# RMSNorm row sums on TensorE in a two-layer network kernel: the matmuls that sum squares get stationaries of 32 columns on four groups of columns, where they had 128

## The chip, the cores and the metric

The kernel runs on one core of one Trainium2 chip. The metric is the device time of one execution in microseconds (us), lower is better. The time before is a median of 2035.81 us over three runs (2034.48 to 2036.75).

## What is computed

Two layers over 1024 tokens of 1024 features, in float32, then a last norm:

```python
for layer in range(DEPTH):                       # DEPTH = 2
    h = rmsnorm(x, mix_norm[layer])
    y = sliding_window_attention(h, ...) if layer % 2 == 0 else hgrn2_recurrence(h, ...)
    x = x + y
    h = rmsnorm(x, mlp_norm[layer])
    x = x + jnp.square(jax.nn.relu(h @ w_up)) @ w_down    # 1024 -> 4096 -> 1024
return rmsnorm(x, final_norm)
```

`rmsnorm(x, gain)` is `x * rsqrt(mean(x*x over features) + 1e-5) * gain`. The recurrence has one more such norm of its output. The mean over features, one number for each token, is what the change is about.

## The kernel before

**Layout.** Activations lie with 128 features on the partitions and 512 tokens (a half, `hf` 0 or 1) along the free axis, so one half of `x` is 8 tiles of 128x512. Matmuls on float32 data go as three float32r products (`mm3`): the data are split into a high and a low part (tiles `a`, `t` for activations, `wh` and `wl` for weights). The accumulators in PSUM are the tiles `p` and `q`, four of each. The MLPs and the recurrence's projections use Strassen products, and their operands go to DRAM (`d`) and back.

**The means.** `sum_squares` (L545) squares the eight tiles of a half on ScalarE and adds them on VectorE into one tile of 128x512: the sum over 8 features for each partition and token. `token_rstd` (L555) then has to add over the 128 partitions. It does so on TensorE, one block of 128 tokens at a time: the stationary is the block of the summed squares (128 partitions x 128 tokens), the one moving column is `self.mean`, a 128x1 tile that holds 1/1024, and the result is a column of 128 partitions in a `q` tile, the mean of squares of each token. Both operands are float32, and the trace holds two MATMUL and two LDWEIGHTS records (two passes) for each such matmul. A chain of five small VectorE and one small ScalarE instructions on 128x4 tiles (`sm`) makes 1/sqrt of it, and `spread` or a scalar operand uses it.

`token_rstd` is called 13 times: twice before the attention (`scaled`), four times in `weigh` (two for each MLP), twice for the recurrence's input (`hgrn_first`, `hgrn`), twice for its output (`hgrn_out`), each time for a half of 512 tokens and so with 4 matmuls; and three times in `final`, where the sum comes in two parts (seven tiles, then the eighth), that is 8 matmuls for the first half and 4 for each of two quarters. That makes 56 matmuls, 112 passes. In the very last call three and four matmuls of the identity with itself (`warm`, written to `q` tiles that nobody reads) stand behind the two parts.

**Matmuls with 32 columns.** The recurrence (`recurrence`) already has matmuls whose stationary has 32 columns: each writes 32 partitions of a PSUM tile, and four of them in turn write the four groups of 32 partitions. They come in visits of 64 matmuls (128 passes) or 32, four visits for each of the 8 heads, with ordinary matmuls in between.

**What sets the order.** Nothing runs when it is written: every instruction is recorded (`Schedule.add`), and `Schedule.forward` plans all engines with costs in ns that stand in the code. On each engine the ready operation of lowest rank goes next. On TensorE the rank is the place in which the operation was recorded, less a lead; on the other engines it is, from the second pass on, the latest start that `backward` finds. `order` makes four passes and keeps the plan that ends first by its own costs. A change of form, from matmuls on the whole array (`"whole"`) to matmuls on groups of columns (`"columns"`), counts 200 ns in the plan (`DRAIN`). All instructions are then issued from one line (L434), so the profile names them by tiles: the norm's matmuls are `q<-c,t 128x1` (in `hgrn_out`, `q<-c,a 128x1`), the 32-column ones of the recurrence are `q<-t,t` with 128*32.

Of the kernel before, what the change touches and what calls it, by code (L numbers as in the profile page):

```python
# [17 lines left out]
P = 128  # L18
# [24 lines left out]
QB = 32  # L43
# [5 lines left out]
class View:  # L49


    def __init__(self, buf, steps=(), part=None):
        self.buf, self.steps, self.part = buf, steps, part
# [103 lines left out]
class Schedule:  # L157


    def __init__(self):  # L160
        self.ops, self.tags, self.lead = [], {}, 0

    def tile(self, pool, bufs, shape, dtype, tag, name):
        return View(Buf(pool, bufs, shape, dtype, tag, name))
# [1 line left out]
    def add(self, ways, outs, ins, tail=0.0, form=None, table=None):  # L166

        op = Op()
        op.ways, op.tail, op.form, op.table, op.index = ways, tail, form, table, len(self.ops)
        lead = self.lead  # L170
        if any(isinstance(v, View) and v.buf.tag == "p" for v in ins):
            lead = max(lead, EVACUATE)
        op.late = None
        op.rank, op.after, op.first = (len(self.ops) - lead, len(self.ops)), [], []
        before, bufs = set(), {}
        for views, writes in ((ins, False), (outs, True)):
            for v in views:
                if isinstance(v, View):
                    bufs[v.buf] = None
                    before.update(v.buf.conflicts(v.part, writes))  # L180
        for views, writes in ((ins, False), (outs, True)):
            for v in views:
                if isinstance(v, View):
                    v.buf.note(op, v.part, writes)
        before.discard(op)
        op.bufs, op.before = list(bufs), list(before)
        op.banks = [v.buf for v in ins if isinstance(v, View) and v.buf.tag in "pq"]
        for b in op.bufs:
            if b.uses == 0:
                op.first.append(b)  # L190
                self.tags.setdefault((id(b.pool), b.tag), []).append(b)
            b.uses += 1
            b.users.append(op)
        for o in before:
            o.after.append(op)
        self.ops.append(op)
# [183 lines left out]
class Net:  # L380
# [174 lines left out]
    def token_rstd(self, acc, inner=1.0, outer=1.0, n=TH, keep=False, more=(), busy=(0, 0)):  # L555

        ps = self.psum("q")
        nb = n // P
        parts = [acc, *more]
        for i, z in enumerate(parts):  # L560
            for j in range(nb):
                first, last = (j == 0, j == nb - 1) if more else (True, True)
                self.mm(ps[:, j : j + 1], z[:, j * P : j * P + P], self.mean, i == 0 and first, i == len(parts) - 1 and last, P, 2,
                        skip_group_check=bool(more))
            if busy[i > 0]:
                self.warm(self.ident, busy[i > 0], "q", 217.0)
        v, y, z = (self.t(F32, (P, BPH), "sm")[:, :nb] for _ in range(3))
        self.ts("DVE", v, ps[:, :nb], inner, EPS, ALU.mult, ALU.add, 4)
        self.act(y, v, AF.Sqrt, 4)
        self.op("DVE", self.nc.vector.reciprocal, [y], [y], 100, y, y)  # L570
        self.tt("DVE", z, y, y, ALU.mult, 4)
        self.stt(z, v, -0.5 * outer, z, ALU.mult, ALU.mult, 4)
        if keep:
            y, r = self.const((P, BPH)), y
        else:
            r = y
        self.stt(y, z, 1.5 * outer, r, ALU.add, ALU.mult, 4)
        return y
# [1362 lines left out]
```

## Time and profile before

| | |
|---|---|
| three runs, median | 2035.81 us |
| the profiled execution's own time | 2035.75 us |
| its span, first to last instruction | 2034.0 us |
| mean granted TensorE clock | 0.998 |
| TensorE matmul (PE) busy | 2017.9 us, 99% |
| VectorE (DVE) busy | 1841.3 us, 91% |
| ScalarE (ACT) busy | 1310.6 us, 64% |
| moved to and from HBM | 243 GB/s over the span |

In the profile PE is TensorE's matmuls and PEld its loads of stationaries, which overlap them. A line of a group gives the engine, the operation, out<-in by tile names, the shape, the count, the busy time in us and the mean length of one in ns, and the idle time before them. Busy time is the union of the instructions' times, so overlapping ones share it. A line of the timeline gives the start and the length in us, then the instructions that are merged in it. Ends of matmuls are modelled and overlap the next one's start; what a matmul costs is seen from starts, not from lengths.

### The profile page before, as it was taken

The numbers are of one execution on the slowest core, as the hardware profiler recorded it, in microseconds if no ns is written. First come the engines' busy times: TensorE is split into PE (matmuls) and PEld (weight loads), VectorE is DVE, ScalarE is ACT, GpSimd is POOL, SyncE is SP. The second block draws the span as 40 slices with busy tenths as digits, with TensorE's granted clock in tenths as the row PEclk, the third lists the DMA queues.
The fourth block names the chain that finished last, engine by engine and source line by source line (L and its number), as shares of the span: only waits on it lengthen the run. The fifth ranks groups of instructions, "written<-read, shape, count | busy, mean of one in ns | idle before, by whom it ended". The sixth has DMA issues, their size and how long they took to land.

```text
span 2034.0 us, 40229 instructions
## 1 busy us (share of the span) xinstructions
PE 2017.9 (99%) x13964; PEld 1714.3 (84%) x13964; DVE 1841.3 (91%) x3738; ACT 1310.6 (64%) x2759; POOL 64.4 (3%) x152
## 2 busy tenths in 40 slices
PE   9999999999999999999999999999999999999998
PEld 7878888899998888888888888878888999888887
DVE  8899979899999979889989999989999999997985
ACT  7577977667676544657666666666767667544573
POOL 4030000000000000000000000000000000000000
PEclk9999999999999999999999999999999999999999
DMA  6212478778789987755888889979798788997812
GB/s 229 78 51 73 137 254 264 248 263 281 269 289 309 319 279 236 255 171 182 283 285 284 284 292 310 329 254 316 243 299 296 258 295 285 322 319 233 269 53 83
DMA packets 275420, 497.40 MB, mean 245 GB/s; under 512 B 30992, under 2 KB 36368, under 8 KB 275216
## 3 DMA queue, kind: packets, MB, share of 16 engines
q1 hardware_dynamic: 275072, 494.81, 72.5%
q8 instruction: 110, 1.80, 0.4%
q14 instruction: 94, 0.77, 0.1%
q10 hardware_dynamic: 144, 0.02, 0.0%
HBM read 394.57 MB, written 100.14 MB: 243 GB/s over the span
## 4 chain that ended last, share of the span: by engine, by line
PE 92%; DVE 5%; DMA 1%; ACT 1%; issue 1%; SPq 0%; DVEq 0%; ACTq 0%
PE p L434 50%; PE q L434 42%; DVE t L434 2%; DVE a L434 1%; DVE wl L434 1%; DVE m L434 1%; ACT t L434 0%; DVE sm L434 0%; DMA a<-in_x 0%; DMA d<-t 0%; DMA t<-in_x 0%; DMA d<-a 0%; ACT a L434 0%; SPq L434 0%; ACT m L434 0%
## 5 line engine op out<-in xcount | busy, mean ns | idle before, releaser
L434 PE MATMUL p<-a,wh 128*128 128x512 f32 (+1 forms) x2832 | 781.9, 361 | 1.3 <-ACT t L434 0.8
L434 PE MATMUL q<-a,wh 128*128 128x512 f32 x2020 | 626.5, 390 | 0.4 <-DVE a L434 0.2
L434 PEld LDWEIGHTS p<-a,wh 128*128 128x128 f32 x2832 | 503.3, 189 | 82.0 <-ACT t L434 1.3
L434 PE MATMUL p<-a,wl 128*128 128x512 f32 (+1 forms) x1416 | 504.1, 359 | 0.7 <-DVE wl L434 0.7
L434 PEld LDWEIGHTS q<-a,wh 128*128 128x128 f32 x2020 | 374.7, 188 | 74.9 <-DVE a L434 0.8
L434 PE MATMUL q<-a,wl 128*128 128x512 f32 x1008 | 392.0, 389 | 0.0
L434 ACT CAST wh<-m 128x512 fp32r<-128x512 f32 (+1 forms) x354 | 212.8, 605 | 204.1 <-PE q L434 96.3
L434 ACT CAST wh<-wr 128x512 fp32r<-128x512 f32 (+1 forms) x324 | 194.5, 603 | 164.8 <-PE p L434 106.8
L434 PEld LDWEIGHTS p<-a,wl 128*128 128x128 f32 x1416 | 266.5, 189 | 39.2 <-DVE wl L434 1.4
L434 DVE TENSOR_TENSOR wl<-m,wh 128x512 fp32r<-128x512 f32 (+1 forms) x354 | 236.0, 671 | 37.1 <-ACT wh L434 31.4
L434 DVE TENSOR_TENSOR wl<-wr,wh 128x512 fp32r<-128x512 f32 (+1 forms) x324 | 215.4, 669 | 18.7 <-ACT wh L434 16.9
L434 DVE TENSOR_TENSOR a<-t,a 128x512 fp32r<-128x512 f32 (+2 forms) x321 | 212.0, 679 | 17.7 <-PE q L434 7.8
L434 DVE TENSOR_TENSOR t<-t,t 128x512 f32<-128x512 f32 (+3 forms) x376 | 218.7, 605 | 7.4 <-ACT t L434 4.2
L434 PEld LDWEIGHTS q<-a,wl 128*128 128x128 f32 x1008 | 189.3, 188 | 38.9
L434 ACT ACTIVATE t<-t 128x512 f32<-128x512 f32 x288 | 179.3, 631 | 52.2 <-DVE t L434 44.5
L434 ACT CAST a<-t 128x512 fp32r<-128x512 f32 (+1 forms) x241 | 142.4, 607 | 30.4 <-DVE t L434 10.3
L434 ACT COPY t<-q 128x512 f32<-128x512 f32 (+2 forms) x254 | 111.8, 442 | 29.4 <-PE q L434 23.4
L434 DVE TENSOR_TENSOR t<-t,p 128x256 f32<-128x256 f32 x288 | 116.6, 418 | 15.0 <-PE p L434 11.2
L434 PE MATMUL p<-wh,a 128*128 128x512 f32 x384 | 125.6, 396 | 1.0 <-ACT a L434 0.6
L434 DVE TENSOR_TENSOR m<-wr,wr 128x512 f32<-128x512 f32 (+1 forms) x184 | 120.0, 654 | 1.0 <-DMA wr<-in_down 0.6
L434 DVE TENSOR_TENSOR a<-a,a 128x512 fp32r<-128x512 f32 (+2 forms) x151 | 101.7, 685 | 7.6 <-ACT a L434 3.6
L434 ACT CAST a<-a 128x512 fp32r<-128x512 f32 x136 | 82.6, 619 | 22.6 <-DVE a L434 19.2
(131 smaller groups left out, 2454.7 us busy)
## 6 DMA issues: line engine op xcount, KB each, us to landing
t<-d SPq DMA_DIRECT2D x592, 256.0 KB, 4.6
a<-d SPq DMA_DIRECT2D x318, 256.0 KB, 4.6
d<-t SPq DMA_DIRECT2D x290, 256.0 KB, 3.4
wr<-in_down SPq DMA_DIRECT2D x224, 256.0 KB, 4.2
wr<-in_up SPq DMA_DIRECT2D x172, 256.0 KB, 4.2
wr<-in_win SPq DMA_DIRECT2D x68, 256.0 KB, 5.2
d<-a SPq DMA_DIRECT2D x64, 256.0 KB, 3.5
wr<-in_wqkv SPq DMA_DIRECT2D x48, 256.0 KB, 2.7
```

The source lines that it names most:

```text
L434: fn(*[place(a) for a in args], **{k: place(v) for k, v in kw.items()})
```

## The change

Each of the 56 matmuls becomes four. The stationary is now 32 tokens of the summed squares (`QB` is 32), the moving column is the same, and the result goes to 32 partitions of the same column of the `q` tile, so that four matmuls in a row write the four groups of 32 partitions. They are recorded as `"columns"`, with a cost of 32 x 1.28 / 2.4 + 4 = 21 ns in the plan, where 128 columns counted 128 x 2 / 2.4 + 4 = 111 ns. All matmuls of a part of the sum now have the rank of the part's first (`group`).

```diff
     def __init__(self):
-        self.ops, self.tags, self.lead = [], {}, 0
+        self.ops, self.tags, self.lead, self.group = [], {}, 0, None
...
         op.late = None
-        op.rank, op.after, op.first = (len(self.ops) - lead, len(self.ops)), [], []
+        at = len(self.ops) if self.group is None else self.group
+        op.rank, op.after, op.first = (at - lead, len(self.ops)), [], []
...
         for i, z in enumerate(parts):
+            self.s.group = len(self.s.ops)
             for j in range(nb):
                 first, last = (j == 0, j == nb - 1) if more else (True, True)
-                self.mm(ps[:, j : j + 1], z[:, j * P : j * P + P], self.mean, i == 0 and first, i == len(parts) - 1 and last, P, 2,
-                        skip_group_check=bool(more))
+                for b in range(0, P, QB):
+                    self.mm(ps[b : b + QB, j : j + 1], z[:, j * P + b : j * P + b + QB], self.mean, i == 0 and first,
+                            i == len(parts) - 1 and last, QB, 1.28, "columns", skip_group_check=bool(more))
+            self.s.group = None
             if busy[i > 0]:
                 self.warm(self.ident, busy[i > 0], "q", 217.0)
```

Since the plan's costs change, the plan changes with them: on all five engines instructions change places with their neighbours all through the program, while what is issued is otherwise the same (32-column matmuls of the recurrence included). In the last head of the recurrence, the four visits of 32-column matmuls had 21, 15 and 15 rows of ordinary matmuls between them; now it is 14, 13 and 16.

On TensorE at the first norm, in the projections before the attention, four matmuls of the norm (`q_443`) stood one by one between products of the projection before:

```order
L434 MATMUL p_234<-wh_349,a_341 128x512
L434 MATMUL q_443<-c_69,t_227 128x1
L434 MATMUL p_234<-wl_370,a_341 128x512
L434 MATMUL q_443<-c_69,t_227 128x1
L434 MATMUL p_234<-wh_349,a_381 128x512
L434 MATMUL q_443<-c_69,t_227 128x1
L434 MATMUL p_239<-wh_349,a_341 128x512
L434 MATMUL q_443<-c_69,t_227 128x1
L434 MATMUL p_239<-wl_370,a_341 128x512
```

At the same place there are now sixteen in one row (the same norm's tile is called `q_410` here):

```order
L435 MATMUL p_234<-wh_327,a_353 128x512
L435 MATMUL q_410<-c_69,t_227 32x1 x16
L435 MATMUL p_239<-wh_327,a_319 128x512
L435 MATMUL p_239<-wl_341,a_319 128x512
L435 MATMUL p_239<-wh_327,a_353 128x512
```

So the group keeps the matmuls of one norm together, and the ordinary products stand in front of them and behind.

On TensorE at the norm of the recurrence's output (`hgrn_out`, first half), three matmuls of the norm and then the fourth stood among 128x128 products of the last head:

```order
L434 MATMUL q_18446<-t_18282,m_18451 128x128
L434 MATMUL q_18446<-t_17894,t_18036 128x128
L434 MATMUL q_18468<-c_69,a_12790 128x1 x3
L434 MATMUL q_18446<-t_18282,m_18451 128x128
L434 MATMUL q_18446<-t_17894,t_18036 128x128
L434 MATMUL q_18446<-t_18282,m_18451 128x128
L434 MATMUL q_18468<-c_69,a_12790 128x1
L434 MATMUL q_18484<-a_18120,wh_18182 128x512
```

Now one of the sixteen stands ahead of one such product and fifteen behind it:

```order
L435 MATMUL q_18539<-t_18373,m_18544 128x128
L435 MATMUL q_18539<-t_17986,t_18024 128x128
L435 MATMUL p_17908<-a_18105,wl_18273 128x512
L435 MATMUL q_18561<-c_69,a_12864 32x1
L435 MATMUL q_18539<-t_18373,m_18544 128x128
L435 MATMUL q_18561<-c_69,a_12864 32x1 x15
L435 MATMUL q_18588<-a_18157,wh_18267 128x512
```

The norm still comes in two pieces, now of one and of fifteen matmuls, with one product of the head between them instead of three.

On TensorE at the end of the program, the last norm's two parts (`t_25917`, then `t_26609`) had seven matmuls of the identity (`c_67` alone) between them:

```order
L434 MATMUL p_23312<-a_26165,a_26246 128x256
L434 MATMUL q_26596<-c_69,t_25917 128x1 x2
L434 MATMUL q_26601<-c_67 128x128 x3
L434 MATMUL q_26606<-c_67 128x128 x4
L434 MATMUL q_26596<-c_69,t_26609 128x1 x2
L434 MATMUL q_26625<-c_67,sm_26618 128x128 x2
```

Now six stand between them and one behind:

```order
L435 MATMUL p_23428<-a_26279,a_26362 128x256
L435 MATMUL q_26752<-c_69,t_26037 32x1 x8
L435 MATMUL q_26763<-c_67 128x128 x3
L435 MATMUL q_26770<-c_67 128x128 x3
L435 MATMUL q_26752<-c_69,t_26768 32x1 x8
L435 MATMUL q_26770<-c_67 128x128
L435 MATMUL q_26793<-c_67,sm_26786 128x128 x2
```

One matmul of the identity thus moved from ahead of the last part to behind it.

## The prediction

> **What bounds the kernel now.** I read the page's totals first, then the chain that ended last, then the waits of TensorE, then the timeline at the places that the change touches.
>
> ```profile
> span 2034.0 us, 40229 instructions
> PE 2017.9 (99%) x13964; PEld 1714.3 (84%) x13964; DVE 1841.3 (91%) x3738; ACT 1310.6 (64%) x2759; POOL 64.4 (3%) x152
> PE 92%; DVE 5%; DMA 1%; ACT 1%; issue 1%; SPq 0%; DVEq 0%; ACTq 0%
> ```
>
> TensorE is busy for all but 16 us of 2034, and 92% of the chain is its own. What is taken from its sequence of matmuls comes off the time, as long as the others keep up. The waits of TensorE show how little it waits now; these are the longest, in us in total, times, longest:
>
> ```profile
> PE q L434 <- issue: 2.9, 2, 2.8
> PE q L434 <- DVE sm L434: 1.4, 1, 1.4
> PE p L434 <- DVE t L434: 1.1, 1, 1.1
> PE p L434 <- ACT t L434: 0.8, 1, 0.8
> PE p L434 <- DVE wl L434: 0.7, 2, 0.4
> PE p L434 <- ACT a L434: 0.6, 1, 0.6
> ```
>
> Of these 1.1 + 0.8 + 0.7 + 0.6 = 3.2 us are waits for another engine's data, the 1.4 us is the very last norm, and 2.8 us is one wait for nothing that the profile shows, of which more below. The profiled execution took 2035.75 us, 1.75 us more than its span; the median of the runs is 2035.81 us, so the sum can be made against 2035.75.
>
> **The change, part by part.** First what goes. The groups say that the norms hold 96 + 16 = 112 passes:
>
> ```profile
> L434 PE MATMUL q<-c,t 128*128 128x1 f32 x96 | 11.6, 236 | 0.0
> L434 PE MATMUL q<-c,a 128*128 128x1 f32 x16 | 2.0, 235 | 0.0
> ```
>
> Their busy time overlaps the neighbours, so I take the price from starts in the timeline, at a norm of the recurrence's input, and at the first norm, where the matmuls stand singly:
>
> ```profile
> 905.25 0.39 PE L434 MATMUL p<-a,wl 128*128 128x512 f32 x1
> 905.48 0.94 PE L434 MATMUL q<-c,t 128*128 128x1 f32 x8
> 906.29 5.97 PE L434 MATMUL p<-a,a 128*128 128x512 f32 x25
> ...
> 20.95 0.48 PE L434 MATMUL p<-wl,a 128*128 128x512 f32 x1
> 21.27 0.28 PE L434 MATMUL q<-c,t 128*128 128x1 f32 x2
> 21.40 0.47 PE L434 MATMUL p<-wh,a 128*128 128x512 f32 x1
> ```
>
> A product of 512 columns occupies 905.48 - 905.25 = 0.23 us. The eight passes of one norm hold the array from 905.48 to 906.29, 0.81 us. The product behind a norm's pass takes 21.27 - 20.95 = 0.32 us instead of 0.23, another 0.09. So one norm of a half costs 0.90 us now, and singly (0.13 + 0.09 for two passes) it is 0.22 x 4, the same.
>
> Then what comes. No row of this profile shows a 32-column stationary with one moving column. The nearest are the recurrence's visits, with 16 and 32 moving columns: a full one of 128 passes, and a stray one of two.
>
> ```profile
> 965.68 0.39 PE L434 MATMUL p<-a,wl 128*128 128x512 f32 x1
> 966.00 1.31 PE L434 MATMUL q<-t,t 128*32 128x32 f32 x128
> 967.24 0.73 PE L434 MATMUL p<-a,wh 128*128 128x512 f32 x2
> 967.81 0.40 PE L434 MATMUL p<-a,wl 128*128 128x512 f32 x1
> ...
> 1276.04 0.23 PE L434 MATMUL q<-t,t 128*32 128x16 f32 x2
> 1276.20 0.73 PE L434 MATMUL p<-a,wh 128*128 128x512 f32 x2
> ```
>
> Going in costs 966.00 - 965.68 = 0.32, that is 0.09 over a product's 0.23. From a visit's start to the product behind it 2 passes take 0.16 us and 128 take 1.24, so a pass more costs (1.24 - 0.16) / 126 = 8.6 ns, and 32 passes take 0.16 + 30 x 0.0086 = 0.42. The two products behind take 0.57 instead of 0.46, 0.11 more. A norm of a half will cost 0.09 + 0.42 + 0.11 = 0.62 us, 0.28 less than now. For one moving column I keep the same 8.6 ns a pass: lower it could be by little, since four passes must still load four blocks of weights; the upper end is passes that don't overlap, a rival below. The Trainium skill, TensorE: Matmul & The Clock Gate, section "Wait — 56ns, not 53.3ns?", says that starts of matmuls are never closer than about 25 ns however few columns move. By that a norm would take 0.16 + 30 x 0.025 = 0.91 and cost 1.11, more than now; the row of 128 passes in 1.24 us, 9.7 ns each, is against it for matmuls on four groups of columns.
>
> Now the sum, over 13 calls. Nine of the ten calls for a half stand in one visit: 9 x -0.28 = -2.5. The tenth, in the norm of the recurrence's output, is split in the order into one matmul and fifteen. It was split before as well, and two passes cost 0.22 us in a row or singly, so it costs 0.90 now; then a second visit of two passes adds 0.09 + 0.16 + 0.11 to the 0.62, less the 2 x 0.0086 that it takes over, 0.96: +0.06. The last norm's first half has both parts in a row, 16 passes now and 64 then, and each of its quarters has parts of 4 passes, then 16:
>
> ```profile
> 1995.88 1.84 PE L434 MATMUL q<-c,t 128*128 128x1 f32 x16
> 1997.58 0.85 PE L434 MATMUL p<-a,a 128*128 128x256 f32 x5
> ...
> 2010.06 0.50 PE L434 MATMUL q<-c,t 128*128 128x1 f32 x4
> 2010.43 1.80 PE L434 MATMUL p<-a,a 128*128 128x256 f32 x13
> ```
>
> The half costs 1.70 + 0.09 = 1.79 now, and 0.09 + (0.16 + 62 x 0.0086) + 0.11 = 0.89 then, -0.90. A quarter's part costs 0.37 + 0.09 = 0.46 now, and 0.09 + (0.16 + 14 x 0.0086) + 0.11 = 0.48 then: three such parts, +0.06. The fourth is on the path that ends the program:
>
> ```profile
> 2023.26 1.81 PE L434 MATMUL q<-c 128*128 128x128 f32 x14
> ...
> 2024.01 0.42 ACT L434 ACTIVATE t<-a 128x256 f32<-128x256 f32 x1 [2.06 <-DVE a L434]
> ...
> 2024.90 0.51 PE L434 MATMUL q<-c,t 128*128 128x1 f32 x4
> ```
>
> The square that it needs is done at 2024.43, yet it starts at 2024.90, behind fourteen passes of the identity that take 1.64 us, 0.12 each. One of the seven matmuls moves behind it, which frees two passes, 0.23 us, against 0.09 for going in: about -0.15, and I take nothing for a shorter last pass. Sum: -2.5 + 0.06 - 0.90 + 0.06 - 0.15 = -3.43 us, 2035.75 - 3.43 = 2032.3 us, which is -0.17%.
>
> Nothing waits longer for a norm: it ends earlier by up to 0.28 us, or with the second visit 0.06 us later. What hides the added work of issue (448 passes in place of 112, each a LDWEIGHTS and a MATMUL, 672 instructions more) is the lead with which TensorE's instructions are fetched; where that cover is thin is in the first two rivals. The rest of the order moves too, on all engines. Its instructions are the same, so I cost it at nothing, with the 3.2 us of waits above as the scale on both sides, the third rival.
>
> **The rivals.** In the last head of the recurrence the visits of 32-column matmuls come close together, and TensorE loses time there for no reason that the waits name:
>
> ```profile
> 1327.89 1.33 PE L434 MATMUL q<-t,t 128*32 128x16 f32 x128
> ...
> 1331.10 0.39 PE L434 MATMUL p<-a,wl 128*128 128x512 f32 x1
> 1331.71 0.73 PE L434 MATMUL p<-a,wh 128*128 128x512 f32 x2 [0.22 <-issue]
> ...
> 1333.30 1.27 PE L434 MATMUL q<-t,t 128*32 128x16 f32 x121
> 1337.33 0.25 PE L434 MATMUL q<-t,t 128*32 128x16 f32 x7 [2.75 <-issue]
> ...
> 1338.00:1342.00 4.00, 4.00 (x13) 3.10 (x12) 3.34 (x10) 2.47 (x7) 0.00 (x0) 0.57 1.06 388
> ...
> q8 instruction: 110, 1.80, 0.4%
> ```
>
> A visit stops after 121 of 128 passes for 2.75 us, and then the granted clock is 0.57 from 1338 to 1342 (in the row of windows it stands behind the engines' busy times, and the DMA share, 1.06, full, behind it): 0.43 x 4 = 1.7 us is lost. With 0.38 at 1331 this place costs 2.75 + 0.38 + 1.7 = 4.8 us. I read it as instructions that came late: queue 8 fetched 110 packets of 1.80 MB / 110 = 16.4 KB, and 13964 + 13964 TensorE instructions over 110 are 254 a packet, 64 bytes each. A full visit is 256 instructions in 1.24 us, a whole packet, while ordinary products need 254 x 0.115 = 29 us for one. The Trainium skill, Runtime: NRT & Kernel Launch, section "Instruction fetch mechanics", also has blocks of 16 KiB, but says that fetching them is mostly hidden; by that the wait is something else and stays as it is, at 2032.3. No run here shows yet which.
>
> First rival, the place heals: 672 more instructions, some 2.6 packets, shift where a packet ends in a visit, and the late one may fall between visits. Then 2032.3 - 4.8 = 2027.5. Against it: the order is denser there now, 14 and 13 rows between the first three visits where there were 21 and 15.
>
> Second rival, on the other side, the same mechanism: one fetch more comes late in those visits. Price 2.75 + 1.7 = 4.45 each: 2036.8, slower than before, with one, and 2041.2 with two. It decides from the point where visits follow each other within 5.4 us, as 1333.30 follows 1327.89: 14 or 13 rows of 0.23 us with a visit of 1.24 and 0.2 for switching make 4.7 and 4.4 us. For it: the DMA queues are full there, and now two gaps in a row are so short.
>
> Third, the new order gives the gain back: VectorE is busy 91% of the span, and its instructions are in another order everywhere. If the waits for other engines double, that is +3.2 us, 2035.5, no change; if they vanish, 2029.1.
>
> Fourth, the change doesn't do what it says. The groups of the recurrence's visits, for 16 and for 32 moving columns:
>
> ```profile
> L434 PE MATMUL q<-t,t 128*32 128x16 f32 x2560 | 27.6, 185 | 2.8 <-issue 2.8
> L434 PE MATMUL q<-t,t 128*32 128x32 f32 x768 | 9.8, 199 | 0.0
> ```
>
> It may be that with one moving column, the four groups don't work side by side; then a pass costs 4 x 8.6 = 34 ns, a norm 0.09 + 0.16 + 30 x 0.034 + 0.11 = 1.38, 0.48 more than now, and with fourteen times that 2035.75 + 6.7 = 2042.5. The rows speak against it: 27.6 / 2560 = 10.8 ns for 16 columns and 9.8 / 768 = 12.8 for 32, so fewer columns don't cost more. The Trainium skill's 25 ns, with 0.21 us more for each of fourteen norms, would give 2038.7, an estimate by that page, and I count it with this rival.
>
> **How the numbers follow.** Forecast as summed, 0.40: 2032.3, with 2 us on both sides for small moves of the order. The place heals, 0.20: 2027.5. One fetch more late 0.09, two 0.04. The order gives it back, 0.21. No overlap, 0.06. The range from 2027.0 to 2038.0 us leaves out most of the fourth, two late fetches, and the case of healing with a better order. About 0.2%, 4 us, is what a measurement of this kernel can tell from no change: faster means under 2031.7. That takes all of healing and nearly half of the forecast, 0.20 + 0.19 = 0.39; slower means over 2039.9, the fourth, two late fetches, and a little of the third with waits that more than double, 0.12; the rest is 0.49.
>
> **What would show it.** Right: 448 passes of 32x1 with 0.42 us from a norm's start to the product behind it; the half of the last norm in 0.69 us; no longer waits for `sm`; TensorE's waits for data near 3 us. The last head decides the rest: a visit there with a gap named "issue", a lower clock behind it. Wrong: passes of over 15 ns, or gaps in front of the norms because sixteen matmuls stand where products could have gone; or waits for VectorE of many us in the MLPs, where TensorE now has none.

## The result and the profile after

The changed kernel takes 2023.87 us (median of six), the kernel before 2034.76 us on the same chip. One of the six took 2848.59 us at a mean granted clock of 0.654 and is left out of all that follows; the other five lie from 2022.9 to 2025.82, with a median of 2023.63. Their ratio to before is 0.9945, 95% interval [0.9934, 0.9956]: 0.55% faster, where 0.17% was forecast, and below the range of 2027.0 to 2038.0.

The profiled execution took 2024.11 us. Its page has, in this order, the span, the engines' busy times, the instruction queue and the chain that ended last:

```profile
span 2022.3 us, 40876 instructions
...
PE 2012.0 (99%) x14300; PEld 1705.6 (84%) x14300; DVE 1837.8 (91%) x3738; ACT 1308.5 (65%) x2759; POOL 62.5 (3%) x152
...
q8 instruction: 113, 1.85, 0.4%
...
PE 97%; DVE 1%; DMA 1%; issue 0%; ACT 0%; SPq 0%; DVEq 0%
```

TensorE still sets the time, now with 97% of the chain where it had 92%, in spite of 336 more passes and three more packets of instructions. Its waits (us in total, times, longest; the whole answer):

```profile
PE p L435 <- DVE t L435: 1.1, 1, 1.1
PE q L435 <- DVE sm L435: 1.0, 1, 1.0
PE q L435 <- issue: 0.7, 2, 0.4
PE p L435 <- ACT t L435: 0.6, 1, 0.6
PE p L435 <- DVE wl L435: 0.3, 1, 0.3
PE q L435 <- DVE m L435: 0.2, 1, 0.2
```

The 2.9 us of "issue" are down to 0.7, the very last norm from 1.4 to 1.0. The waits for data are 1.1 + 0.6 + 0.3 + 0.2 = 2.2 now. To compare, the list before has to be taken whole as well; behind the six lines that the prediction shows it goes on with

```profile
PE p L434 <- DVE a L434: 0.5, 2, 0.3
PE q L434 <- ACT m L434: 0.5, 1, 0.5
PE q L434 <- DVE a L434: 0.4, 2, 0.2
```

so that it had 3.2 + 1.4 = 4.6 us, and the prediction's 3.2 was not all of it. The norms themselves, first a norm of the recurrence's input, then the first half of the last norm:

```profile
902.73 0.39 PE L435 MATMUL p<-a,wl 128*128 128x512 f32 x1
903.05 0.43 PE L435 MATMUL q<-c,t 128*32 128x1 f32 x32
903.41 1.88 PE L435 MATMUL p<-a,a 128*128 128x512 f32 x7
...
1985.96 0.71 PE L435 MATMUL q<-c,t 128*32 128x1 f32 x64
1986.60 1.70 PE L435 MATMUL p<-a,a 128*128 128x256 f32 x12
```

Going in takes 903.05 - 902.73 = 0.32 us, 0.09 over a product, as forecast. The 32 passes take 0.36 us from their start to the next product (0.42 forecast), the 64 take 0.64 (0.69 forecast). The price of a pass came as forecast: the trace has 262 ns from the first to the last of the 32 starts, 31 steps of 8.45 ns on average (8.6 forecast). The row of 0.43 us and the mean length of one pass, 173 ns, say the same within their rounding:

```profile
L435 PE MATMUL q<-c,t 128*32 128x1 f32 x384 | 5.4, 173 | 0.0
```

What was too high is the term for the first two passes. It was taken from a lone visit of two, 0.16 us, and in the trace that one has 52 ns from the first pass to the second and 113 ns to the product. A row of 32 has 8.45 ns a step and 100 ns to the product: 0.26 + 0.10 = 0.36. And in the last head, where time was lost before:

```profile
1321.85 1.31 PE L435 MATMUL q<-t,t 128*32 128x32 f32 x128
...
1326.49 1.41 PE L435 MATMUL q<-t,t 128*32 128x16 f32 x128
...
1330.99 1.04 PE L435 MATMUL q<-t,t 128*32 128x16 f32 x95
1332.46 0.57 PE L435 MATMUL q<-t,t 128*32 128x16 f32 x33 [0.43 <-issue]
...
1336.82 0.95 PE L435 MATMUL q<-t,t 128*32 128x32 f32 x64
```

```profile
1330.00:1334.00 4.00, 3.57 (x138) 2.75 (x136) 3.97 (x11) 2.23 (x5) 0.00 (x0) 1.00 0.92 325
```

The visits follow each other as closely as the order had shown, and yet the third stops for 0.43 us instead of 2.75, after pass 95 instead of 121. The clock (the third number from the end of a row of windows) stays at 1.00, here and behind it.

**Where the 11.6 us went.** For this I took from both traces the median time from one matmul's start to the next, for each kind of matmul and its two neighbours, and summed these medians over each kernel's sequence; what a step takes beyond its median is put down to what ended it. That gives, of the 2033.97 - 2022.33 = 11.6 us of span (rounded; tail is the last norm and what follows it):

| | before | after | difference |
|---|---|---|---|
| sequence at its medians, with small scatter | | | -3.5 |
| late instructions (gaps named issue, short ones too) | 4.9 | 1.5 | -3.4 |
| the stretch at half clock behind the long gap | 1.55 | 0 | -1.55 |
| waits for other engines' data | 8.2 | 5.6 | -2.6 |
| tail | | | -0.6 |

The third row follows from the second. These are one profiled execution of each; the medians differ by 10.9 us. The levels depend on how small excesses are sorted: when only steps of more than 60 ns over their median are counted, late instructions are 3.8 and 1.4 us and waits 5.1 and 1.9. So the differences of these two rows, -2.4 to -3.4 and -2.6 to -3.2, are good to about a microsecond, and the levels to three or four.

### The profile page after: what moved, and what is told of

It is laid out like the page before. It is cut to its first block, busy times and chain, and to the rows that moved or that the text cites. A ratio compares the mean times of both kernels' runs of the same rounds, so it can differ in the third digit from the quotient of the medians.

```text
span 2022.3 us, 40876 instructions
## 1 busy us (share of the span) xinstructions
PE 2012.0 (99%) x14300; PEld 1705.6 (84%) x14300; DVE 1837.8 (91%) x3738; ACT 1308.5 (65%) x2759; POOL 62.5 (3%) x152
## 3 DMA queue, kind: packets, MB, share of 16 engines
q8 instruction: 113, 1.85, 0.4%
## 4 chain that ended last, share of the span: by engine, by line
PE 97%; DVE 1%; DMA 1%; issue 0%; ACT 0%; SPq 0%; DVEq 0%
PE p L435 53%; PE q L435 44%; DVE t L435 1%; DMA a<-d 0%; DMA a<-in_x 0%; DVE a L435 0%; DMA d<-t 0%; DVE wl L435 0%; DVE m L435 0%; ACT t L435 0%; DVE sm L435 0%; SPq L435 0%; ACT a L435 0%; DVEq L1919 0%; ACT sm L435 0%
```

## The experiments

Two theories stood at first. One: the passes bring about 5 us, and the rest is the order, in two ways: where the packets of instructions end, and how long TensorE waits for data. The rival: the passes alone are worth the whole, since they are shorter than I had costed, or take a wait away that I did not see. A third question was what the gaps named "issue" are.

**Narrow passes in the old order, whole passes in the new.** In the first kernel all engines keep the order of before, and each matmul of a norm is issued as four:

```diff
-                self.mm(ps[:, j : j + 1], z[:, j * P : j * P + P], self.mean, ..., P, 2, ...)
+                self.op("PE", self.narrow, ..., P * 2 / 2.4 + 4, ..., form="whole", ...)
...
+    def narrow(self, out, lhsT, rhs, **kw):
+        for b in range(0, P, QB):
+            self.nc.tensor.matmul(out[b : b + QB], lhsT[:, b : b + QB], rhs, **kw)
```

In the second all engines keep the order of after; the first of four recorded matmuls issues the one with 128 columns, the other three issue nothing:

```diff
-                    self.mm(ps[b : b + QB, j : j + 1], z[:, j * P + b : j * P + b + QB], self.mean, ..., QB, 1.28, "columns", ...)
+                    whole = ps[:, j : j + 1], z[:, j * P : j * P + P], self.mean
+                    self.op("PE", self.nothing if b else self.nc.tensor.matmul, ..., QB * 1.28 / 2.4 + 4, *whole, form="columns", ...)
```

Expected of the first: 

> Before's order on every engine, with each norm matmul issued as four of 32 columns. Theory (the passes give about 5 us by themselves, by starts 0.90 to 0.56 us a norm; the rest of the 10.9 us comes from the late instruction packet in the last head and from waits, which depend on where packets end and on the order): 5 us less than before if the gap in the last head stays, 2029.8, and down to 2025 if the 288 instructions more ahead of it (32 modulo 256) move it off; any gap named issue that is left starts at an instruction whose place in TensorE's stream is 192 to 194 modulo 256. Rival (the new order gives the gain, the passes little): 2033 to 2035.

Expected of the second: 

> After's order on every engine, with the norms' matmuls issued as 128 columns, as before. Theory: 5 us more than after, 2028.9, and up to 5 more if the 288 instructions fewer bring a late packet into the last head again; its waits for data stay those of after. Rival (the order gives nothing, all is the passes): 2034.8, like before.

Measured: old order with narrow passes 2027.95 us, ratio 0.9964 [0.9952, 0.9977]; new order with whole passes 2029.61, 0.9973 [0.9963, 0.9983]; before 2035.44 beside them. So the passes are worth 7.5 us in the old order and 2029.61 - 2023.87 = 5.7 in the new, the order 5.8 with whole passes and 4.1 with narrow ones. By the intervals each of these is good to 2 or 3 us, so that 7.5 and 5.7, or 5.8 and 4.1, are not told apart; the order with whole passes is worth 3.5 to 7.5 us. Neither is the whole. The passes' 7.5 hold more than passes. The third visit of the last head in the old order with narrow passes, and the second and third in the new order with whole ones:

```profile
1330.99 1.15 PE L434 MATMUL q<-t,t 128*32 128x16 f32 x105
1333.41 0.38 PE L434 MATMUL q<-t,t 128*32 128x16 f32 x23 [1.28 <-issue]
```

```profile
1328.35 1.30 PE L435 MATMUL q<-t,t 128*32 128x16 f32 x125
1330.98 0.24 PE L435 MATMUL q<-t,t 128*32 128x16 f32 x3 [1.33 <-issue]
...
1334.32 1.20 PE L435 MATMUL q<-t,t 128*32 128x16 f32 x111
1337.14 0.33 PE L435 MATMUL q<-t,t 128*32 128x16 f32 x17 [1.62 <-issue]
...
1338.00:1342.00 4.00, 4.00 (x12) 3.16 (x12) 2.47 (x8) 2.55 (x8) 0.00 (x0) 0.62 1.05 387
```

In the old order the gap moved from pass 121 to 105 and shrank to 1.28 us, and the clock stayed at 1.00. Six norms stand ahead of it, each with 24 passes or 48 instructions more: 288, which is 32 more than 256, and 32 instructions are the 16 passes by which it moved. In the new order with whole passes there are two gaps and then a clock of 0.62; this profiled execution, 2032.39 us, is the longest of its eight, so its gaps may be more than its median has. By the same account as above, late instructions cost 1.6 us in the first kernel and 4.3 in the second, beside 4.9 before and 1.5 after; waits for data 8.1 and 6.0, beside 8.2 and 5.6. The sequence at its medians is 4.0 us shorter in the first, and in the new order 4.9 shorter with narrow passes than with whole ones.

**The common rank alone, the 32 columns alone.** The third kernel is before with `group`, the fourth is after without it:

```diff
-            self.s.group = len(self.s.ops)
```

Expected of the common rank alone: 

> Only the common rank of a part's matmuls, with 128 columns and the old cost in the plan: the order differs from before in a dozen rows on TensorE. Theory: no change, 2034.8 within 1 us, gap in the last head where it was. Rival (keeping a norm's matmuls together is what helps): 2 us or more less.

Expected of the 32 columns alone: 

> 32 columns without the common rank: the order is nearly that of after. Theory: like after, 2023.9 within 1.5 us, with the gap of the last head under 1 us. Rival (the common rank matters): 2 us or more above after.

Measured: the common rank alone 2035.73 us, 0.9998 [0.9989, 1.0007]; the 32 columns alone 2029.56, 0.9971 [0.9959, 0.9983]. The first came as expected. The second missed its expectation of 2023.9 within 1.5 us, and the rival, that the rank matters, came true. With 128 columns the rank is worth nothing; with 32 it is worth 5.7 us, though the two orders are nearly the same. The difference lies in one place, the first norm, whose matmuls stand one by one between products without the rank. In the timeline of the 32 columns alone, and in its windows there:

```profile
18.39 0.22 PE L435 MATMUL q<-c,t 128*32 128x1 f32 x2
18.54 0.50 PE L435 MATMUL p<-wh,a 128*128 128x512 f32 x1
18.97 0.22 PE L435 MATMUL q<-c,t 128*32 128x1 f32 x2
...
26.58 0.27 PE L435 MATMUL q<-c,t 128*32 128x1 f32 x2
26.78 0.79 PE L435 MATMUL p<-wh,a 128*128 128x512 f32 x1
27.50 0.27 PE L435 MATMUL q<-c,t 128*32 128x1 f32 x2
...
22.00:26.00 4.00, 4.00 (x22) 2.12 (x19) 4.00 (x12) 3.97 (x7) 0.00 (x0) 0.67 0.90 282
26.00:30.00 4.00, 4.00 (x12) 2.61 (x12) 2.54 (x8) 2.27 (x4) 0.00 (x0) 0.50 0.99 358
```

A visit of two passes and a product take 18.97 - 18.39 = 0.58 us, 0.35 more than the product: 0.15 for the passes (18.54 - 18.39), 0.20 for going in and out. After five microseconds of this the granted clock falls to half, and then a visit and a product take 27.50 - 26.58 = 0.92. TensorE is shown busy all the time, and yet the clock falls. The same stretch of the changed kernel, with the norm in one visit of 32 passes:

```profile
22.00:26.00 4.00, 4.00 (x19) 3.30 (x19) 3.97 (x16) 3.95 (x8) 0.00 (x0) 1.00 0.95 326
26.00:30.00 4.00, 4.00 (x20) 3.30 (x19) 4.00 (x14) 3.87 (x7) 0.00 (x0) 1.00 0.83 260
```

Counted from the start, the 101st product of 512 columns starts at 29.52 us there and at 36.48 without the rank: 7.0 us, about the whole difference of the two spans (2028.8 - 2022.3 = 6.5). Of this about 3 us are the clock: three of the six executions without the rank have a mean granted clock of 0.997 and take 2030.62 to 2031.01 us, the other three have 0.999 and take 2027.65 to 2028.51. So in the change the rank is a condition of the gain, not a part of it.

**What a gap named issue is.** Each packet of queue 8 holds 16.4 KB, 256 instructions of 64 bytes. I counted TensorE's instructions in its stream (loads, matmuls and the semaphore instructions between them): each of these gaps in a visit begins at an instruction whose number is 192 to 194 modulo 256. That suggests that the engine came to a packet that had not landed. The test puts instructions in front and leaves everything else: the first of the matmuls that warm the array at the start issues N small ones more, on zeros, whose result nobody reads.

```diff
+    def warmed(self, out, lhsT, rhs, more):
+        for i in range(more):
+            b = i % 4 * QB
+            self.nc.tensor.matmul(out[b : b + QB, :1], lhsT[:, :QB], rhs[:, :1], start=True, stop=True)
+        self.nc.tensor.matmul(out, lhsT, rhs, start=True, stop=True)
```

With 16, 32 and 48 of them there are 64, 128 and 192 instructions more. If packets are late, the gap stands 32, 64 and 96 passes earlier in the visit; if the gap belongs to the place (its data, its buffers), it stays after pass 121. Expected of 64 more in the kernel before: 

> Before, every order the same, with 16 matmuls of 32x1 on zeros (64 instructions, read by nobody) ahead of the first warming matmul. Theory (a packet of 256 TensorE instructions ends at places 192 to 194 modulo 256 of the stream, and the visit that crosses into the next one early waits for it): in the last head's third visit the gap moves 32 passes forward, to after about 89 passes; its length may change, 1 to 3.5 us. Rival (the gap is a wait for data of this place, a landing that the profile does not name): it stays behind the 121st pass, 2.75 us. The start costs up to 1 us more in both.

Of 128 more: 

> The same with 32 such matmuls (128 instructions). Theory: a gap in the third visit after about 57 passes, or none there and one in the visit before; total between 2030 and 2037. Rival: the gap stays behind the 121st pass, time as before plus the cost of the start, up to 1.5 us.

Of 192 more: 

> The same with 48 such matmuls (192 instructions). Theory: the gap, if one is left, after about 25 passes of the third visit or in the second; the clock halves only behind a gap of more than about 2.5 us. Rival: the gap stays behind the 121st pass, the clock halves.

And of 128 more in the kernel after: 

> After, every order the same, with 32 such matmuls (128 instructions) ahead. Theory: its two small gaps (at 1285 and 1332 us, 0.5 and 0.6 us over a pass's step) move away from the passes where they stand, to places 192 to 194 modulo 256; the norms' cost and the waits for data stay, so 2022 to 2029 by what the packets do in the last head. Rival (after's gain in the last head comes from its order alone): gaps stay at the same passes, 2024 to 2025.

The third visit in the kernel before with 64, with 128 and with 192 more instructions (for the last, its fourth visit too):

```profile
1335.06 0.98 PE L440 MATMUL q<-t,t 128*32 128x16 f32 x89
1336.93 0.57 PE L440 MATMUL q<-t,t 128*32 128x16 f32 x39 [0.89 <-issue]
```

```profile
1333.27 0.69 PE L440 MATMUL q<-t,t 128*32 128x16 f32 x58
1335.91 1.18 PE L440 MATMUL q<-t,t 128*32 128x16 f32 x70 [1.96 <-issue]
```

```profile
1332.80 0.43 PE L440 MATMUL q<-t,t 128*32 128x16 f32 x26
1333.68 1.16 PE L440 MATMUL q<-t,t 128*32 128x16 f32 x102 [0.46 <-issue]
1338.44 0.28 PE L440 MATMUL q<-t,t 128*32 128x32 f32 x9
1339.90 0.85 PE L440 MATMUL q<-t,t 128*32 128x32 f32 x55 [1.18 <-issue]
```

121, 89, 58, 26: the gap moves with the count of instructions, 32 passes for each 64, as expected; the first, 0.89 us, is a little shorter than the 1 to 3.5 us expected. The DMA records say the same. In the kernel before, from 1334.4 to 1337.4 us, queue 8 has

```profile
q8 instruction: 1, 0.02, 2.0%
```

and this one packet was transferred from 1335.01 to 1335.97, when the visit had already stopped (1334.58); the visit went on 1.36 us after its end. In the fourteen traces 26 gaps named "issue" stand behind the first 200 us, and each ends 1.2 to 1.6 us after the end of a packet of queue 8. That the gaps are late packets is shown; why a packet is fetched late is not. What they cost changes with the shift: 2033.62, 2032.49 (its profiled execution, 2034.44, is the longest of ten) and 2033.55 us beside 2034.78, ratios 0.9991 [0.9982, 1.0], 0.9987 [0.9978, 0.9997] and 0.9993 [0.9983, 1.0002]. Of the three only 128 instructions more is apart from before by its interval, 0.13% faster for work that does nothing. The kernel after with 128 more takes 2026.76 us, ratio to before 0.9957 [0.9942, 0.9972], where after had 0.9945 [0.9934, 0.9956]: slower by the medians, with intervals that overlap. In it the longest gap stands in an earlier head, two products behind a visit, and one more after pass 46 of the last head's second visit. After pass 31 of the third visit, to which the gap of the kernel after would have moved, there is none: the count says where a gap can stand, not which packet comes late.

```profile
1223.68 1.32 PE L441 MATMUL q<-t,t 128*32 128x16 f32 x128
...
1227.61 0.50 PE L441 MATMUL p<-a,wl 128*128 128x512 f32 x1 [1.93 <-issue]
...
1329.28 0.59 PE L441 MATMUL q<-t,t 128*32 128x16 f32 x46
1331.13 1.04 PE L441 MATMUL q<-t,t 128*32 128x16 f32 x82 [1.27 <-issue]
```

Late instructions cost 5.1 us in its profiled execution instead of 1.5. So a part of the 0.55%, up to the 3.4 + 1.55 us of the account, hangs on where packets happen to end.

**Other plans of the same two kernels.** What is left is the 2.6 us of shorter waits for data, and whether these and the packets belong to the change or to the plan. Four kernels have exactly the instructions of before, or of after, and another number in the plan, so that the order comes out anew:

```diff
-                self.mm(..., P, 2, skip_group_check=bool(more))
+                self.mm(..., P, 1.2, skip_group_check=bool(more))
```

The second has 2.4 there; the third has 2.0 for 1.28 in the kernel after; the fourth has 100 for 200 in `DRAIN`.

Expected of before with 1.2: 

> The kernel before, all instructions the same, but the plan counts a norm's matmul as 128 x 1.2 / 2.4 + 4 = 68 ns instead of 111, so that the plan comes out in another order. Theory A (the order's share of the gain is the luck of a plan: where packets end and how the other engines' data fall): the time scatters by several us either way, 2029 to 2038, with packet gaps between 1.5 and 6 us and waits for data between 6 and 11 us. Theory B (the better order belongs to the change): within 2 us of before, 2033 to 2036.5, waits for data 9 to 11 us.

Of before with 2.4: 

> The kernel before, all instructions the same, but the plan counts a norm's matmul as 128 x 2.4 / 2.4 + 4 = 132 ns instead of 111. Theory A (luck of a plan): anywhere from 2029 to 2038, and not the same as with the other cost. Theory B (the better order belongs to the change): 2033 to 2036.5.

Of after with 2.0: 

> The kernel after, all instructions the same, but the plan counts a 32-column matmul of a norm as 32 x 2.0 / 2.4 + 4 = 31 ns instead of 21. Theory A (luck of a plan): 2022 to 2031, the passes' gain of some 5 us is kept and the rest scatters. Theory B (the better order belongs to the change): 2022 to 2025.5.

Of after with a drain of 100: 

> The kernel after, all instructions the same, but the plan counts 100 ns instead of 200 for a change of form; in the traces it costs 0.09 in and 0.11 out. The visits of the last head stand further apart there (the shortest distance that a packet has grows from 4.1 to 4.8 us by durations from the traces). Theory A (luck of a plan): 2021 to 2031; if the distance decides, no gap named issue above 1 us in the last head and 2021 to 2024. Theory B (the better order belongs to the change): 2022 to 2025.5.

Measured, with the same account of the profiled executions (in us):

| kernel | median | ratio | late instructions | waits for data |
|---|---|---|---|---|
| before | 2034.88 | | 4.9 | 8.2 |
| before, 1.2 | 2032.69 | 0.9992 [0.9983, 1.0001] | 5.6 | 7.2 |
| before, 2.4 | 2032.64 | 0.9988 [0.9979, 0.9998] | 3.8 | 7.1 |
| after | 2023.87 | 0.9945 [0.9934, 0.9956] | 1.5 | 5.6 |
| after, 2.0 | 2023.96 | 0.9951 [0.9936, 0.9965] | 2.4 | 5.3 |
| after, drain 100 | 2023.44 | 0.9945 [0.9931, 0.996] | 1.3 | 6.6 |

(The row of after is that of the result, with before at 2034.76 beside it.) By the medians the plan moves the kernel before by about 2 us, hardly more than the intervals tell from nothing, and the kernel after by half a microsecond. Both expectations were half right: the time of before scatters, as the theory of luck has it (both of its new plans are a little below the 2033 of the other theory), but by less than that gave, and not as far as the new order with whole passes, 2029.61. All three plans of after stay together, as the theory of a better order has it. The sharper part of the last expectation is met as well: with the visits further apart, the one gap of the last head is 0.76 us,

```profile
1320.83 1.31 PE L435 MATMUL q<-t,t 128*32 128x16 f32 x127
1322.90 0.18 PE L435 MATMUL q<-t,t 128*32 128x16 f32 x1 [0.76 <-issue]
```

but the time is that of after: its late instructions are down by 0.2 us from 1.5, and its waits for data are up by 1.0. What in the new plans shortens the waits for data by 0.5 to 2.9 us was not found: their lists of waits differ by tenths in many places, and no single wait carries it.

## Why the prediction was wrong, step by step

**The price of a norm: right in its parts, mis-sized in one.** Going in 0.09, the rows behind 0.11, and a further pass, 8.45 ns for 8.6, came as forecast. The 0.16 for the first two passes was 0.06 too much: a lone visit of two, 52 ns from start to start, does not stand for the beginning of a row. A norm of a half costs 0.56 instead of 0.62, so nine save 9 x 0.34 = 3.1 instead of 2.5; the last norm's half saves 0.95 instead of 0.90, its quarters nothing, and the tail 0.6 instead of 0.15. By these prices the terms give about -4.6 where -3.43 stood; the account gives -3.5 - 0.6 = -4.1, and the old order with narrow passes -4.0 without the tail. Here the Trainium skill, TensorE: Matmul & The Clock Gate, has two sentences: the 25 ns between starts of its section "Wait — 56ns, not 53.3ns?" does not hold for these passes, 8.45 ns each on average; its section "Measured speedup vs the span model", with about 4 ns for each further tile of a packed array, is nearer, and still lower than the 6 or 7 ns that the closest starts of the trace are apart.

**"Its instructions are the same, so I cost it at nothing": this step failed.** The new order is worth 5.8 us with whole passes and 4.1 with narrow ones, more than the scale of 3.2 us that I gave it. I took that scale from the list of waits, of which I summed four lines of seven: the whole has 4.6 us, and it holds only gaps of more than 0.15 us. By starts against medians TensorE lost 8.2 us to data (5.1 by the narrower count), not 3.2. And the scale left out late instructions, which an order moves as well.

**The first rival came true, with other numbers and for its own reason.** It had a chance of 0.20 and a price of 4.8 us: the gap of the last head shrank from 2.75 to 0.43 us and the half clock is gone, 3.4 + 1.55 = 5.0 us. The mechanism, late packets of 256 instructions, is shown by the four kernels with shifted counts and by the packets of queue 8. What I held against it, a denser order in that place, does not decide: in the old order with narrow passes the visits stood as before, and the gap shrank as well, to 1.28 us, with the packet's end after pass 105. Where a packet ends in a visit can be counted before any run, from the order: 192 to 194 modulo 256. I had the packet's size and did not count. What the count does not give is the length of a gap, 0.16 to 2.75 us for the 26. The Trainium skill, Runtime: NRT & Kernel Launch, section "Instruction fetch mechanics", says that the cost of crossing a block is mostly hidden; with 113 packets and 1.5 us in the changed kernel that agrees, and for the visits of the last head in the kernel before, with the DMA share at 1.05 to 1.06 and a gap of 2.75 us, it does not.

**The second rival** did not come in the change: the shortest distances, 4.6 and 4.5 us between the starts of the first three visits, are under the 5.4 that I named as the point, and only one gap of 0.43 us followed. In the new order with whole passes it did come, with 1.33 and 1.62 us and a clock of 0.62. So the distance makes gaps possible, but the point that I gave does not decide.

**The third rival** came on its other sign. It names both, 2029.1 us if the waits vanish, but its chance of 0.21 is for a loss alone; the new order shortened the waits by 2.6 us. **The fourth** is ruled out by 8.45 ns a pass, where it needed 34.

**The range.** I priced healing and a better order as two cases and took one at a time; the range says itself that it "leaves out ... the case of healing with a better order". The two have one cause, since the new order moves both, and they came together: -4.6 of passes, -5.0 of gaps and clock and -2.6 of waits are 2035.75 - 12.2 = 2023.6 (the profiled execution took 2024.11). That is a sum made afterwards from the same two traces, not a second forecast.

## What to carry to other kernels

Where one engine is busy 99% of the time, an edit that makes the planner reorder everything has no free part: cost the order from starts against their medians, not from the list of longest waits, and separate it by running the old order with the new instructions and the new order with the old ones. Short passes on groups of columns pay when they stand in one row, 0.56 us for a norm instead of 0.90, and lose it all when they alternate with whole products. Where hundreds of short instructions follow each other under a full DMA load, count at which instruction a packet of 256 ends, and expect a shift of some hundred instructions to move the time: here by about a tenth of a per cent, by the medians, down in one kernel and up in the other.

## What the runs showed of the hardware that was not expected

The granted clock fell to half without any idle time of TensorE in the records: in the 32 columns alone it was 0.67 from 22 to 26 us and 0.50 from 26 to 30, while two passes and one product alternated. And behind gaps the clock did not follow one length. It fell after 2.75 us before, 2.48 with the rank alone, 1.33 and 1.62 in the new order with whole passes, 1.96 in before with 128 instructions more, and 1.93 in the kernel after with 128 instructions more, so the 2.5 us named in the expectation of 192 more is no limit:

```profile
1226.00:1230.00 4.00, 2.39 (x8) 1.97 (x9) 2.75 (x8) 1.35 (x4) 1.42 (x6) 0.86 0.60 186
```

It did not fall after 1.72 and 2.15 us in before with 1.2:

```profile
1337.04 0.37 PE L434 MATMUL q<-t,t 128*32 128x16 f32 x19 [2.15 <-issue]
...
1338.00:1342.00 4.00, 4.00 (x79) 3.13 (x77) 3.98 (x10) 2.83 (x8) 0.00 (x0) 1.00 1.02 364
```

The clock records of the kept traces go further than these rows. In all fourteen, every change of the granted clock lies a whole number of 3.413 us after the first one. Idle time must then be counted within one such stretch: the gap of 2.15 us, which did not lower the clock, is cut by a boundary into 1.17 and 0.98 us, and the one of 1.72 into 0.63 and 1.09, while of the gaps of 2.48, 1.96 and 1.93 us, which did, 2.48, 1.85 and 1.93 lie in one stretch. Idle time alone does not decide even so: 1.62 us in a stretch went with a fall (the new order with whole passes), and 1.73 us, a wait for ScalarE at 553 us in before with 64 instructions more, did not. A count that parts them is that of the moving columns (512 for a product of 128x512, 1 for a pass of a norm) of all matmuls that start in a stretch. Between 15 and 2000 us the fourteen traces have six stretches at the full clock with a fall at their end, and these have 1504 to 3088 columns, the one without idle time in the 32 columns alone among them; the other 8131 have 3328 or more. This was found in the traces afterwards, with a narrow margin, and no run was made to test it.
